# Twenty-four extra rows on SyncE's queue between two tile loads of a batch norm

## The chip, the cores and the metric

The kernel runs on one core of a Trainium2 chip. The metric is the device time of one execution in microseconds, and the time of a kernel is the median of its runs.

## The reference

The input `x` has the shape (32, 256, 128, 128) in float32. Each of the 256 channels is normalized with given statistics, so the whole computation is one multiplication and one addition per element with numbers that depend on the channel alone:

```python
def reference(x, gamma, beta, running_mean, running_var):
    eps = 1e-5
    ...  # each parameter reshaped to (1, 256, 1, 1)
    return gamma * (x - mean) / np.sqrt(var + eps) + beta
```

The input has 537 MB and the output as much.

## The kernel before

The channels are put on the 128 partitions, so `x` becomes 64 tiles (`NT`) of 128 rows; a row is one channel of one image, 16384 numbers or 64 KiB, and a tile is 8 MiB. Three tiles (`NBUF` = 3) fit in the on-chip memory, as `bufs[0]` to `bufs[2]`; tile i uses buffer i modulo 3 and is changed in place.

Loads are issued by SyncE on its queue (q1 in the profile), stores by ScalarE on its own (q10). Both queues are served by the same 16 DMA engines. At the start SyncE issues, in this order: the left half of tile 0 (L90, semaphore `early`), the four parameter vectors into `rows`, 16 rows of 1 KiB each (L93), the right half of tile 0 (L97, `first[0]`), and tiles 1 and 2 whole (L99, `first[1]` and `first[2]`). None of these waits for anything, except that the first parameter load waits for the memset of `rows` (L91). While the data come in, VectorE and ScalarE turn the parameters into `scale_t` and `shift_t`, one column for each half of the channels (L109 to L126).

For each later tile VectorE handles the first columns in two instructions (L132: 1696 columns, then up to 14976) and ScalarE the rest (L143); for tile 0 VectorE takes the left half and ScalarE the right. ScalarE then waits for VectorE's part and issues the store of the tile (L171). Before its part of tile i it waits until the store of tile i - 1 has landed, except for tile 0 and the last two (L168). SyncE's loop over the later loads (L161 to L164) waits for two things: the buffer's old tile must be stored (`gone(i - NBUF)`), and VectorE must have done the first part of tile i - 1 (`vfirst`), which needs that tile's load to have landed. So in mid-run about one load and one store are under way at any time.

Tile 0 is not treated until its halves have landed: VectorE's first part waits for `early`, ScalarE's for `first[0]`. Tile 2 is awaited by VectorE and ScalarE through `first[2]`.

Of the kernel before, what the change touches and what calls it, by code (L numbers as in the profile page):

```python
# [10 lines left out]
NHEAD = 3  # L11
VFIRST = 1696
VMOST = 14976
VHEAD = 8192
VLAST = 9216


@with_exitstack
def kernel(
# [9 lines left out]
    nc = tc.nc  # L29
# [14 lines left out]
    xr = x.rearrange("n (cb p) h w -> (n cb) p (h w)", p=P)  # L44
# [5 lines left out]
    bufs = [data.tile([P, HW], f32, name=f"t{s}", tag=f"t{s}") for s in range(NBUF)]  # L50
# [12 lines left out]
    loaded = [tc.alloc_semaphore(f"loaded{s}") for s in range(NBUF)]  # L63
    stored = [tc.alloc_semaphore(f"stored{s}") for s in range(NBUF)]
    early = tc.alloc_semaphore("early")
    first = [tc.alloc_semaphore(f"first{s}") for s in range(NHEAD)]
    vfirst = tc.alloc_semaphore("vfirst")
    vdone = tc.alloc_semaphore("vdone")
# [5 lines left out]
    with tc.tile_critical():  # L74
# [20 lines left out]
                inst._wait_ge(vec, zeroed)  # L95
            inst.then_inc(fetched, 16)
        nc.sync.dma_start(out=bufs[0][:, right], in_=xr[0][:, right]).then_inc(first[0], 16)  # L97
        for i in range(1, NHEAD):
            nc.sync.dma_start(out=bufs[i][:], in_=xr[i]).then_inc(first[i], 16)  # L99

        def landed(i):
            if i < NHEAD:
                return first[i], 16
            s = i % NBUF
            before = 1 if s < NHEAD else 0
            return loaded[s], 16 * (i // NBUF + 1 - before)
# [6 lines left out]
        for q in range(NQ):  # L113
# [3 lines left out]
            out=std_t[:],  # L117
            in_=var_t,
# [11 lines left out]
        def vector_part(i, first_col, end):  # L130
            t, cb = bufs[i % NBUF], i % NCB
            return nc.vector.tensor_scalar(  # L132
                out=t[:, first_col:end],
                in0=t[:, first_col:end],
                scalar1=scale_t[:, cb : cb + 1],
                scalar2=shift_t[:, cb : cb + 1],
                op0=mybir.AluOpType.mult,
                op1=mybir.AluOpType.add,
            )

        def scalar_part(i, first_col):
            t, cb = bufs[i % NBUF], i % NCB
            return nc.scalar.activation(  # L143
                out=t[:, first_col:],
                in_=t[:, first_col:],
                func=mybir.ActivationFunctionType.Identity,
                bias=shift_t[:, cb : cb + 1],
                scale=scale_t[:, cb : cb + 1],
            ).then_inc(adone, 1)

        def gone(i):
            return stored[i % NBUF], 16 * (i // NBUF + 1)
# [3 lines left out]
        for i in range(1, NT):  # L156
            vector_part(i, 0, VFIRST)._wait_ge(*landed(i)).then_inc(vfirst, 1)
            vector_part(i, VFIRST, VLAST if i == last else VMOST).then_inc(vdone, 1)

# [6 lines left out]
        for i in range(NT):  # L166
            if 0 < i < NT - 2:
                nc.scalar.wait_ge(*gone(i - 1))  # L168
            scalar_part(i, VHEAD if i == 0 else VLAST if i == last else VMOST)._wait_ge(*landed(i))
            nc.scalar.wait_ge(vdone, i + 1)  # L170
# [37 lines left out]
```

## Time and profile before

| | |
|---|---|
| median of 3 runs | 2485.43 us (2484.16 to 2489.99) |
| the profiled execution | 2487.8 us, with a span of 2486.0 us |
| VectorE busy | 526.0 us (21%), 138 instructions |
| ScalarE busy | 111.8 us (4%), 66 instructions |
| moved by DMA | 1073.85 MB, mean 432 GB/s over the span |
| packets on q1 (loads) | 9488, 536.94 MB |
| packets on q10 (stores) | 9216, 536.88 MB |
| a tile's load or store, median from issue to landing | 37.4 us or 37.0 us |
| half of tile 0, issue to landing | 16.4 us |

The span goes from the first to the last instruction of the core; the profiled execution's own time has 1.8 us around it. The row of digits marked DMA gives the mean busy share of the 16 DMA engines in 40 equal slices of the span, in tenths. In a list of waits, each line has the engine and line that waited, what it waited for, the sum in us, how often, and the longest. In a table of windows, the columns are the stretch, its length, the busy time of each engine with its number of instructions, the clock, the share of DMA and the GB/s moved. The trace also holds one record for each single transfer of a DMA engine, with its queue, start, duration and size; a whole row of a tile is one such transfer of 64 KiB.

### The profile page before, as it was taken

What the parts mean: (1) busy time and instruction counts of PE and PEld (TensorE: products, weight loads), DVE (VectorE), ACT (ScalarE), POOL (GpSimd) and SP (SyncE); (2) the same over time, 40 slices, a digit from 0 to 9 for tenths busy, and PEclk for the clock granted to TensorE, in tenths of its full rate; (3) what the DMA queues carried; (4) which work ended last, traced back from release to release, by engine and by line L of the source; (5) the groups of instructions that cost most, each with busy time, mean ns of one, the idle gap of its engine ahead of it and who ended that gap; (6) DMA issues with size and microseconds to landing.
All of it is one profiled execution on the core that took longest, in us unless ns stands there. A gap on an engine that the chain in (4) does not pass through costs nothing.

```text
span 2486.0 us, 578 instructions
## 1 busy us (share of the span) xinstructions
DVE 526.0 (21%) x138; ACT 111.8 (4%) x66; POOL 0.2 (0%) x4
## 2 busy tenths in 40 slices
DVE  2121221221212212122121221212212122121220
ACT  1000000000000000000000000000000000000001
POOL 0000000000000000000000000000000000000000
DMA  9999999999999999999999999999999999999999
GB/s 406 428 431 438 433 428 439 437 433 429 438 429 432 437 436 427 433 432 433 433 438 428 437 436 427 437 436 428 434 437 437 428 437 437 431 433 436 437 429 405
DMA packets 18708, 1073.85 MB, mean 432 GB/s; under 512 B 2128, under 2 KB 2192, under 8 KB 2192
## 3 DMA queue, kind: packets, MB, share of 16 engines
q1 hardware_dynamic: 9488, 536.94, 50.1%
q10 hardware_dynamic: 9216, 536.88, 49.8%
q14 instruction: 4, 0.03, 0.0%
HBM read 536.94 MB, written 536.87 MB: 432 GB/s over the span
## 4 chain that ended last, share of the span: by engine, by line
DMA 93%; DVE 4%; another core or an unknown queue 2%; ACT 0%; issue 0%; SPq 0%; DVEq 0%
DMA t<-in_x_dram 92%; DVE t L132 3%; DMA rows<-in_running_mean_dram 0%; ACT t L143 0%; DVE turned L110 0%; SPq L93 0%; DVE rows L91 0%; DVE par L114 0%; ACT std_t L116 0%; DVE rstd_t L123 0%; DVE shift_t L126 0%; DVE scale_t L124 0%; DVE ms_t L125 0%; DVE eps_t L109 0%
## 5 line engine op out<-in xcount | busy, mean ns | idle before, releaser
L132 DVE TENSOR_SCALAR t<-t,scale_t,shift_t 128x13280 f32<-128x13280 f32 (+2 forms) x127 | 522.5, 4156 | 1921.4 <-DMA t<-in_x_dram 1921.3
L143 ACT ACTIVATE t<-t,shift_t,scale_t 128x1408 f32<-128x1408 f32 (+1 forms) x64 | 110.3, 1723 | 2335.6 <-DMA out_dram<-t 2272.5
L110 DVE STREAM_TRANSPOSE turned<-rows 32x1024 f32<-32x1024 f32 x1 | 1.2, 1232 | 11.8 <-DMA rows<-in_running_mean_dram 11.8
L116 ACT ACT_TABLE_LOAD x1 | 1.3, 1283 | 0.9 <-SPq L74 0.9
L91 DVE MEMSET rows<- 32x1024 f32 x1 | 0.9, 912 | 1.2 <-SPq L74 1.2
L116 ACT ACTIVATE std_t<-par,eps_t 128x2 f32<-128x2 f32 x1 | 0.3, 295 | 14.0 <-DVE par L114 14.0
L114 DVE COPY par<-turned 32x8 f32<-32x8 f32 x4 | 0.6, 162 | 0.1
L123 DVE RECIPROCAL rstd_t<-std_t 128x2 f32<-128x2 f32 x1 | 0.2, 166 | 0.4 <-ACT std_t L116 0.4
L124 DVE TENSOR_TENSOR scale_t<-par,rstd_t 128x2 f32<-128x2 f32 x1 | 0.2, 161 | 0.0
L126 DVE TENSOR_TENSOR shift_t<-par,ms_t 128x2 f32<-128x2 f32 x1 | 0.2, 161 | 0.0
L125 DVE TENSOR_TENSOR ms_t<-par,scale_t 128x2 f32<-128x2 f32 x1 | 0.2, 160 | 0.0
L192 POOL MEMSET const-bfloat16-1.0<- 128x1 bf16 x1 | 0.1, 101 | 0.0
L192 POOL MEMSET const-uint8-127<- 128x1 uint8 x1 | 0.1, 101 | 0.0
L192 POOL MEMSET const-float32-0.0<- 128x1 f32 x1 | 0.1, 98 | 0.2 <-issue 0.2
L192 POOL MEMSET const-float32-1.0<- 128x1 f32 x1 | 0.1, 98 | 0.0
L109 DVE MEMSET eps_t<- 128x1 f32 x1 | 0.1, 59 | 0.1
## 6 DMA issues: line engine op xcount, KB each, us to landing
t<-in_x_dram SPq DMA_DIRECT2D x2, 4096.0 KB, 16.4
out_dram<-t ACTq DMA_DIRECT2D x64, 37.0
t<-in_x_dram SPq DMA_DIRECT2D x63, 37.4
rows<-in_running_var_dram SPq DMA_DIRECT2D x1, 16.0 KB, 11.2
rows<-in_gamma_dram SPq DMA_DIRECT2D x1, 16.0 KB, 11.0
rows<-in_beta_dram SPq DMA_DIRECT2D x1, 16.0 KB, 10.8
rows<-in_running_mean_dram SPq DMA_DIRECT2D x1, 16.0 KB, 10.6
```

Source lines behind the costliest of these rows:

```text
L91: zeroed = step(nc.vector.memset(rows[:], 0.0))
L109: step(nc.vector.memset(eps_t[:], eps))
L110: step(nc.vector.transpose(out=turned[:], in_=rows[:]), fetched, 16 * NPAR)
L114: placed = step(nc.vector.tensor_copy(out=flat[q * B : (q + 1) * B], in_=blocks[:, :, q, 0]))
L116: nc.scalar.activation(out=std_t[:], in_=var_t, func=mybir.ActivationFunctionType.Sqrt, bias=eps_t[:], scale=1.0,)._wait_ge(vec, placed).t ...
L123: step(nc.vector.reciprocal(out=rstd_t[:], in_=std_t[:]), act, 1)
L124: step(nc.vector.tensor_mul(out=scale_t[:], in0=gamma_t, in1=rstd_t[:]))
L125: step(nc.vector.tensor_mul(out=ms_t[:], in0=mean_t, in1=scale_t[:]))
L126: ready = step(nc.vector.tensor_sub(out=shift_t[:], in0=beta_t, in1=ms_t[:]))
L132: return nc.vector.tensor_scalar(out=t[:, first_col:end], in0=t[:, first_col:end], scalar1=scale_t[:, cb : cb + 1], scalar2=shift_t[:, cb ...
L143: return nc.scalar.activation(out=t[:, first_col:], in_=t[:, first_col:], func=mybir.ActivationFunctionType.Identity, bias=shift_t[:, cb : ...
L192: nc = _bacc.Bacc("TRN2", target_bir_lowering=False, num_devices=1)
```

## The change

Between the load of tile 0's right half and the load of tile 1, SyncE issues three small loads into the buffer of tile 2. Each takes a quarter of a row (4096 numbers, 16 KiB) from every fourth row: 12 rows of the first quarter, 8 rows of the second, 4 rows of the third. They bring the same data to the same places as tile 2's whole load does later. Each has a semaphore of its own, and SyncE waits for all three before it issues the load of tile 2, which is now a statement of its own behind the loop. The rest of the kernel is the same.

```diff
+GROUPS = (12, 8, 4)
+PIECE = 4096
...
     early = tc.alloc_semaphore("early")
+    aside = [tc.alloc_semaphore(f"aside{g}") for g in range(len(GROUPS))]
...
         nc.sync.dma_start(out=bufs[0][:, right], in_=xr[0][:, right]).then_inc(first[0], 16)
-        for i in range(1, NHEAD):
+        rest = NHEAD - 1
+        for g, k in enumerate(GROUPS):
+            cut = slice(g * PIECE, (g + 1) * PIECE)
+            nc.sync.dma_start(
+                out=bufs[rest][0 : 4 * k : 4, cut], in_=xr[rest][0 : 4 * k : 4, cut]
+            ).then_inc(aside[g], 16)
+        for i in range(1, rest):
             nc.sync.dma_start(out=bufs[i][:], in_=xr[i]).then_inc(first[i], 16)
+        for g in range(len(GROUPS)):
+            nc.sync.wait_ge(aside[g], 16)
+        nc.sync.dma_start(out=bufs[rest][:], in_=xr[rest]).then_inc(first[rest], 16)
```

## The prediction

> **What bounds the kernel.** I read the page first: how busy each engine is, what the DMA engines moved over the span, and the two queues' shares.
>
> ```profile
> span 2486.0 us, 578 instructions
> ...
> DVE 526.0 (21%) x138; ACT 111.8 (4%) x66; POOL 0.2 (0%) x4
> ...
> DMA  9999999999999999999999999999999999999999
> ...
> q1 hardware_dynamic: 9488, 536.94, 50.1%
> q10 hardware_dynamic: 9216, 536.88, 49.8%
> ```
>
> VectorE and ScalarE are mostly idle; the 16 DMA engines are busy for 50.1 + 49.8 = 99.9% of the span, half with loads (q1, SyncE's queue), half with stores (q10, ScalarE's). One DMA engine therefore moves 536.88 MB / 16 in 0.498 x 2486 us of stores, 27.1 GB/s. The trace's records of single transfers say the same: a 64 KiB row takes 2418 ns, which no row of either direction undercuts, and 97% of the 16256 rows are within 3 ns of that. The kernel is bound by each DMA engine's own speed.
>
> Then the waits of the compute engines and of SyncE, and the chain at the end, to see whether a late DMA engine can leave others without work.
>
> ```profile
> DVE t L132 <- DMA t<-in_x_dram: 1921.3, 63, 35.4
> ...
> SPq L163 <- DMA out_dram<-t: 1427.0, 61, 68.9
> SPq L164 <- DVE t L132: 958.4, 61, 16.0
> ```
>
> ```profile
> 2413.45 42.43 DMA t<-in_x_dram
> 2455.88 0.03 issue
> 2455.90 6.36 ACT t L143
> ```
>
> Everybody waits for transfers. In mid-run a load starts at 1020.27 us and a store at 1045.02, the next load 39 us after the first: the two boundaries lie 25 and 14 us apart, so where one queue runs dry for a moment the other has at least 14 us of rows left. Only the last store is different: it is issued at 2462.29, when ten of the sixteen engines had been idle for about 0.5 us; these end at 2482.5, the latest at 2484.3.
>
> Last, how much time is lost to rows slower than 2418 ns, because a change of order can win only that. The windows show one such stretch, the start of tile 1's load.
>
> ```profile
> 23.50:34.35 10.85, 0.00 (x0) 7.21 (x1) 0.00 (x0) 1.00 1.00 387
> 1990.00:2240.00 250.00, 55.12 (x13) 9.36 (x6) 0.00 (x0) 1.00 1.00 433
> ```
>
> The last column is GB/s: 387 while all 16 engines read in step (five rows each at about 2714 ns, begun within 0.5 us of each other), 433 in a stretch without slow rows. Over the whole run the rows above 2418 ns cost 5.4 us per DMA engine: 1.5 in those five rows, the rest nearly all in loads (later loads 3.7). With every row at its least the data need 16256 / 16 x 2.418 + 16 x 1.213 (tile 0's half rows) = 2476.1 us; the first starts 2.0 us into the span, the span ends 1.7 us after the last, and the profiled execution is 2487.8 us against a span of 2486.0. That gives a floor of 2481.6 on the profiled execution, 6.2 below it. This execution lies 2.4 us above the median of 2485.43 and inside the runs' 2484.16 to 2489.99; I carry differences over to the median.
>
> **The change, part by part.**
>
> *Three more DMAs.* They add 24 rows of 16 KiB, 393 KB on 1073.85 MB. At 27.1 GB/s a row is 0.60 us of one engine. Spread evenly that is 1.5 rows, 0.9 us; all on one engine it is 14.5 us. Nearest row: the four parameter loads, 16 rows of 1 KiB each, show 64 packets of 46 ns that start within 1.0 us in all; one engine alone would need 2.9 us, so rows are dealt out over the engines. I take one row per engine: 12 engines get one row, 8 of them a second, 4 a third. Four DMA engines then have 1.8 us more to do, four 1.2, four 0.6, four nothing. [...]
>
> *What the 1.8 us cost at the end.* An engine with 1.8 us more ends 1.8 us later, unless it was one of the early ones: ends differ by 1.8 us and the early ones had 0.5 us idle, so the cost is 0 if the lag falls on early engines and 1.8 if on late ones. Who is late is made by slow reads along the way and I cannot tell it; I take 1.2.
>
> *SyncE's issues and its waits.* Three more issues of about 0.4 us (L93's duration) put tile 1's load at about 5.7 us instead of 4.4. That is covered: its rows cannot start before tile 0's right half is done at 23.5 us. SyncE then waits for all three pieces, which sit directly behind tile 0's right half and land at about 26 us; tile 2's load is queued behind this wait, and all later loads. It goes out at some 27 us instead of 4.9, behind tile 1's load, which keeps each engine busy from 24 to 26 us on for eight rows: cover to 43 us at least, 16 us to spare. The store of tile 0 (31.79 us) is on another queue. [...] ScalarE's start on tile 0 does not move, as the pieces lie behind the half it waits for.
>
> *The five slow rows.* They ran with 0.5 us between first and last engine; now the groups are 0.6 us apart. If closeness made them slow, 1.5 us comes back; if reading alone did, nothing. I take half, -0.7. [...]
>
> *Slow reads later.* After 100 us a read that begins with 8 or more engines reading and ends with fewer than 12 of them costs 22 ns over 2418 on the mean of 2417 such reads; all others 1.2 ns. An engine that alternates reads and writes, 0.6 us behind the next group, makes the two later of four groups end their reads while the others write, so they pay 22 ns per read. But each payment pushes the engine further back, and after some 2.4 us it reads where most others write and pays nothing: the loss ends itself. The run before, which starts in step, is spread over the whole row by 600 us and paid 3.7 us in this way. I take a little more, +0.6, with bounds of -3.7 (no slow reads) and +7.4 (the later groups never drift out: 504 reads x 22 ns = 11.1 us, less 3.7).
>
> Sum: 1.2 - 0.7 + 0.6 = +1.1 us; 2487.8 to 2488.9 for the profiled execution, 2485.43 to **2486.5** for the median. A difference of 0.3% (7.5 us) is about what a measurement of this kernel can tell from no change.
>
> **The rivals.**
>
> *Gain.* The shift takes the slow rows away: -1.5 and -3.7 with +1.2 of lag, -4.0 us, 2481.4. For it: 1.5 of the 2.2 us lost in the first 250 us fell into rows that began within 0.5 us of each other. Against it: 1990 to 2240 us has no slow row although eleven of the sixteen engines stay within 0.7 us of each other there (rows under way at 2000 us), and the stretches with slow reads are ones in which the engines were spread. Even all of it stays under 0.3%; more than that needs a base that itself ran like the slowest of its three (2489.99).
>
> *Slower: the later groups stay where they pay.* +7.4 + 1.8 = +9.2, 2494.6. It decides from about 85% of the reads of the last group: (7.5 - 1.8 + 3.7) / 11.1. For it: reads are slow exactly at a half-and-half mix, which the shift sets up on purpose from the start, and the engines with most extra bytes are the last group. Against it: the drift just told.
>
> *The pieces are not dealt out* as taken, many rows falling on one engine: up to +14.5 us, 2499.9. Against it stand the parameter rows.
>
> *The shift is there but dies at once*, since the first slow reads move engines by as much as it does (one read took 3869 ns): 2485.4 to 2487.2. I count this with the forecast.
>
> **How the numbers follow.** Forecast 0.44 (2484 to 2489, all within 0.3%); gain 0.28, of which 0.06 beyond 0.3%; later groups stay 0.22, of which 0.18 beyond 0.3%; rows on few engines 0.06. So faster 0.06, same 0.44 + 0.22 + 0.04 = 0.70, slower 0.18 + 0.06 = 0.24. The range goes from 2480.5, just under the gain, to 2495, just over the price of the staying groups; outside remain the rows on few engines and the ends of the other cases.
>
> **What would show it.** In the profile after: tile 1's load issue at about 5.7 us and tile 2's at about 27 us; three issues of 192, 128 and 64 KB landing by 27 us; GB/s in the first 11 us of tile 1's load between 387 and 433; the DMA row still 9 everywhere; the spread of the engines' last ends 2 to 4 us. The prediction is wrong if mean GB/s in mid-run is under 430 with slow reads throughout, if rows run below 2418 ns, or if DMA engines stand idle while SyncE waits at the new waits.

## The result: 0.19% slower, and a profile that does not show why

The changed kernel has a median of 2490.68 us against 2485.36 us for the kernel before, 22 runs each. The ratio is 1.0019 with a 95% interval of 1.0013 to 1.0025, that is 4.7 us (3.2 to 6.2). It is inside the range and within 0.3%, but four times the +1.1 us of the sum. Here and below a median is over all runs of a kernel, while a ratio compares only the runs within 1.5% of their kernel's fastest, which leaves out, among others, four of the six of big_64k, two of the six of equal_64k and three of the twelve of after_v0 (2563 to 2566 us, not profiled).

First the page and the start of the timeline of the profile after. In the timeline the columns are the start in us, the duration, the engine, the line and the instruction.

```profile
span 2485.8 us, 582 instructions
...
DMA  9999999999999999999999999999999999999999
...
q1 hardware_dynamic: 9536, 537.33, 50.1%
q10 hardware_dynamic: 9216, 536.88, 49.8%
```

```profile
4.41 2.24 SPq L104 DMA_DIRECT2D t<-in_x_dram  x3
6.69 0.44 SPq L108 DMA_DIRECT2D t<-in_x_dram  x1
...
26.00 0.33 SPq L111 DMA_DIRECT2D t<-in_x_dram  x1
31.25 0.37 ACTq L183 DMA_DIRECT2D out_dram<-t  x1
```

The DMA engines are busy for the same 99.9%. The 48 more packets (9536 for 9488) are the 24 rows of 16 KiB and 24 records of 4 bytes: the trace has 12, 8 and 4 semaphore steps for the three DMAs, where the load of tile 1 has 16. Twelve of the 24 rows were under way at once at 23.2 us, so they were dealt out over the engines; that it was one row of a DMA per engine, as the prediction took it, fits these counts. The three issues took 2.24 us in place of the 1.3 that I had put, so tile 1's load goes out at 6.69 us and not at 5.7; tile 2's goes out at 26.00, near the 27 forecast. The start of tile 1's load and the last store, in windows (the last two columns are the busy share of the DMA engines and GB/s), and SyncE's new wait:

```profile
23.50:34.35 10.85, 0.00 (x0) 7.21 (x1) 0.00 (x0) 1.00 0.99 426
```

```profile
2455.00:2467.00 12.00, 5.27 (x2) 6.36 (x1) 0.00 (x0) 1.00 0.88 382
```

```profile
SPq L110 <- DMA t<-in_x_dram: 18.8, 1, 18.8
```

426 GB/s stand for the 387 of before: the five slow rows are gone. SyncE's 18.8 us at L110 hold up nothing, as tile 1's rows were queued (DMA share 1.01 from 26 to 36 us). At the end the DMA engines are busy for only 88% of the 12 us around the last store; the same window of the kernel before has:

```profile
2455.00:2467.00 12.00, 5.27 (x2) 6.36 (x1) 0.00 (x0) 1.00 1.00 431
```

These two profiled executions, 2487.8 us before and 2487.56 after, cannot show the loss: one lies above its kernel's median and one below. So I made an account of each profiled execution from the records of single transfers, as a mean per DMA engine: work (all rows at 2418, 1213 or 611 ns for 64, 32 or 16 KiB), what slow rows took beyond that, and idle time. (The 7.3 us of slow rows of the kernel before are the prediction's 5.4, which counted rows of 64 KiB alone, and 1.9 in tile 0's half rows.) With 2.4 to 2.8 us for the ends of the program the terms add up to the measured time in all of them, which makes them comparable. The column "offset" is the time from a store's issue to the next load's landing, read in mid-run; it becomes important below.

| kernel | offset, us | time, us | work | slow rows | idle before the last store | idle elsewhere |
|---|---|---|---|---|---|---|
| before | 12.9 | 2487.80 | 2476.1 | 7.3 | 0.3 | 1.7 |
| changed | 12.9 | 2487.56 | 2477.0 | 4.7 | 1.2 | 2.2 |
| equal_16 | 17.7 | 2488.03 | 2477.9 | 4.5 | 2.6 | 0.5 |
| late_60 | 12.9 | 2483.99 | 2477.0 | 2.2 | 0.5 | 1.8 |
| small_1024 | 8.0 | 2483.92 | 2476.3 | 3.3 | 0.0 | 1.8 |
| held_3 | 22.5 | 2493.58 | 2476.1 | 10.2 | 4.3 | 0.4 |
| after_v0 | 8.0 | 2486.05 | 2477.0 | 4.8 | 0.0 | 1.7 |
| equal_v0 | 8.0 | 2487.04 | 2477.9 | 4.7 | 0.0 | 1.8 |
| before_v0 | 0.8 and 3.2 in turn | 2585.16 | 2476.1 | 81.9 | 0.0 | 24.4 |
| big_64k | 22.5 | 2535.58 | 2479.7 | 39.3 | 8.5 | 5.4 |
| equal_64k | 22.6 | 2544.85 | 2483.3 | 46.0 | 9.1 | 3.6 |

### The profile page after: what moved, and what is told of

Its sections match the earlier page's. It is cut to its first block, busy times and chain, and to the rows that moved or that the text cites. A ratio compares the mean times of both kernels' runs of the same rounds, so it can differ in the third digit from the quotient of the medians.

```text
span 2485.8 us, 582 instructions
## 1 busy us (share of the span) xinstructions
DVE 526.0 (21%) x138; ACT 111.8 (4%) x66; POOL 0.2 (0%) x4
## 3 DMA queue, kind: packets, MB, share of 16 engines
q1 hardware_dynamic: 9536, 537.33, 50.1%
## 4 chain that ended last, share of the span: by engine, by line
DMA 93%; DVE 4%; another core or an unknown queue 2%; ACT 0%; issue 0%; SPq 0%; DVEq 0%
DMA t<-in_x_dram 92%; DVE t L144 3%; DMA rows<-in_running_mean_dram 0%; ACT t L155 0%; DVE turned L122 0%; SPq L96 0%; DVE rows L94 0%; DVE par L126 0%; ACT std_t L128 0%; DVE rstd_t L135 0%; DVE shift_t L138 0%; DVE ms_t L137 0%; DVE scale_t L136 0%; DVE eps_t L121 0%
```

## The first four experiments: is it the shift, the place, or the issues?

**equal_16**: the same three DMAs, but 16 rows in each.

```diff
-GROUPS = (12, 8, 4)
+GROUPS = (16, 16, 16)
```

> Three pieces of 16 rows each in place of 12, 8 and 4: the same three issues, the same wait ahead of tile 2's load, but every DMA engine gets the same 48 KiB (1.8 us) more, so nothing is shifted between the engines. Theory 'lag' (the change costs what the engines with most extra rows have more to do, 1.8 us): 1.8 us over the kernel before. Theory 'slow reads' (the shift between the engines makes more reads slow over the whole run): 1.8 us over before as well, with slow rows as before, the five slow rows at the start of tile 1's load back. Rival 'queue' (the three issues and SyncE's wait cost the time, whoever gets the rows): as the changed kernel, about 5 us over before.

Measured: median 2490.09 us against 2484.09, ratio 1.0023 (1.0014 to 1.0031). No engine is shifted against another and the loss is as large. The shift is not needed for a loss of this size, which speaks against my main rival, the groups that stay where they pay. Part of the loss is a dearer piece: the 48 rows of 16 KiB took 1112 ns on the mean, most 1234 to 1279, twice the 611 ns of the fastest. In late_60, whose 24 pieces of the same size go from device memory to device memory, each took 611. That points to the on-chip side, though those 24 also ran at another time, among other rows. What doubles them was not shown. Three such pieces are 3.3 us per engine where 1.8 had been put, still 2.4 short of the measured 5.7 (the ratio times 2484).

**late_60**: the pieces ahead of tile 60's load, from the input to the output's last tile.

```diff
+            if i == WHEN:        # 60, ahead of the load of tile i
+                for g, k in enumerate(GROUPS):
+                    cut = slice(g * PIECE, (g + 1) * PIECE)
+                    nc.sync.dma_start(
+                        out=outr[last][0 : 4 * k : 4, cut], in_=xr[last][0 : 4 * k : 4, cut]
+                    ).then_inc(aside[g], 16)
...
+            if i == last:
+                for g in range(len(GROUPS)):
+                    nc.scalar.wait_ge(aside[g], 16)
```

> The pieces of 12, 8 and 4 rows are moved from the start to just ahead of tile 60's load, and go from the input to the output's last tile in device memory (overwritten by the last store), so that no load waits for them. The engines are shifted only for the last 6% of the run. 'Lag': 1.8 us over before. 'Slow reads': also about 1.8 us, the remaining 3 us of the changed kernel's loss are gone, since no time is left for slow reads. If the loss is made at the end alone (the last store waits for the latest engine and the shift is paid more than once): about 5 us over before.

Measured: median 2487.64 against 2484.09, ratio 1.0021 (1.0012 to 1.0030), 3.0 to 7.5 us. That is over the 1.8 us of both first theories, by at least 1.2. Its profiled execution, at 2483.99, is the fastest of its eleven and shows nothing of it. What the run does say: a loss of this size does not need 2400 us to build up.

**small_1024**: the same issues and waits, 4 KiB a row.

```diff
-PIECE = 4096
+PIECE = 1024
```

> Pieces of 4 KiB a row in place of 16 KiB: the same issues and waits, a shift of at most 0.45 us between the groups of engines, in the order of the 0.5 us that they differ by anyway. 'Lag': 0.45 us over before, less up to 1 us if the five slow rows go: within 1 us of before. 'Slow reads': close to before too, as the groups stay in step at first. 'Queue': about 5 us over before.

Measured: median 2485.14, ratio 1.0004 (0.9995 to 1.0013). Three issues and SyncE's wait cost nothing that can be told from zero (3.2 us at most by the interval); the cover named in the prediction holds. Its account has no idle time before the last store. Its last load landed at 2449.4 us and its last store went out at 2455.8, and the window around both is full:

```profile
2440.00:2470.00 30.00, 5.27 (x2) 6.36 (x1) 0.00 (x0) 1.00 1.01 437
```

For equal_16, whose last load landed at 2457.8 us and whose last store went out at 2464.2, a window over both reads:

```profile
2455.00:2467.00 12.00, 5.27 (x2) 6.36 (x1) 0.00 (x0) 1.00 0.70 300
```

**big_64k**: whole rows.

```diff
-PIECE = 4096
+PIECE = 16384
...
-            cut = slice(g * PIECE, (g + 1) * PIECE)
+            cut = slice(g, g + 4 * k, 4)
...
-                out=bufs[rest][0 : 4 * k : 4, cut], in_=xr[rest][0 : 4 * k : 4, cut]
+                out=bufs[rest][cut], in_=xr[rest][cut]
```

> Pieces of whole rows, 64 KiB in place of 16 KiB: the groups are shifted by 2.4, 4.8 and 7.2 us, one row each. 'Lag': 7.2 us over before. 'Slow reads': the groups with one and with three rows read while the others write; half of the reads run at a half-and-half mix: 508 reads times 12 to 20 ns, 6 to 10 us of slow reads per engine in place of 3.7, and 7.2 of lag, so 10 to 14 us over before. 'Queue': 5 us over before as in the changed kernel.

Measured: median 2552.55 (2509.67 to 2595.30), 68 us over before; the ratio, 1.0154 (1.0110 to 1.0198), is 38 us (27 to 49). Every theory was far too low. Slow rows took 39.3 us per engine in the profiled execution and idle time 14, while the extra work is 3.6.

**What the timelines had in common.** In small_1024, before and equal_16, around 2010 us, the store's issue (ACTq) and VectorE's start on the next landed load:

```profile
2011.45 0.34 ACTq L183 DMA_DIRECT2D out_dram<-t  x1
2019.49 8.27 DVE L144 TENSOR_SCALAR t<-t,scale_t,shift_t 128x1696 f32<-128x1696 f32 x2 [30.38 <-DMA t<-in_x_dram]
```

```profile
2013.01 0.34 ACTq L171 DMA_DIRECT2D out_dram<-t  x1
2025.87 8.27 DVE L132 TENSOR_SCALAR t<-t,scale_t,shift_t 128x1696 f32<-128x1696 f32 x2 [30.37 <-DMA t<-in_x_dram]
```

```profile
2008.75 0.34 ACTq L183 DMA_DIRECT2D out_dram<-t  x1
2026.45 8.27 DVE L144 TENSOR_SCALAR t<-t,scale_t,shift_t 128x1696 f32<-128x1696 f32 x2 [30.37 <-DMA t<-in_x_dram]
```

The landing comes 8.0, 12.9 and 17.7 us after the store's issue: steps of 4.8 us, one row of each direction (2 x 2418 ns). Within the first 90 us the offset takes one of these values, and in these three it keeps it to the end, since loads and stores both come round every 38.7 us. The larger it is, the later the last load lands against the stores that could fill its time, and the longer the engines idle before the last store (0.0, 0.3 to 1.2 and 2.6 us in the table). From this came a new theory, "offset": the extra rows lie on the loads' queue alone and push the loads' boundaries back against the stores'. These profiles alone do not show it: before and the changed kernel have the same 12.9, and at 12.9 the slow rows differ by 5.1 us from one execution to another (2.2 in late_60, 7.3 in before).

## Four experiments on the offset

**held_3**: no extra rows; the kernel before with one load held once.

```diff
             nc.sync.wait_ge(*gone(i - NBUF))
+            if i == NHEAD:
+                nc.sync.wait_ge(vdone, i)
```

> No extra rows at all: the kernel before, in which SyncE holds the first load of its loop (tile 3) until VectorE has finished tile 2, some 7 us more, once. New theory 'offset', formed from the traces: what counts is by how much the loads' boundaries lie behind the stores'. The time from a store's issue to the next load's landing was 12.9 us before and with the change, 8.0 with 4 KiB pieces and 17.7 with equal pieces, in steps of one row of each direction (4.8 us), and stayed the same from the second load to the end; the larger it is, the longer all DMA engines idle before the last store (mean 0.3, 1.2, 0.0 and 2.6 us). 'Offset' expects 17.7 or 22.5 us here from the start to the end, 2 to 5 us of idle engines before the last store, and 2 to 5 us over before. 'Lag' and 'slow reads', in which the extra rows or the shift between engines cost the time, expect no difference, since there are neither.

Measured: median 2491.39 against 2484.42, ratio 1.0028 (1.0018 to 1.0037). The offset was 8.0 us until the hold, went to 22.5 and stayed:

```profile
2007.90 0.34 ACTq L173 DMA_DIRECT2D out_dram<-t  x1
2030.91 8.27 DVE L132 TENSOR_SCALAR t<-t,scale_t,shift_t 128x1696 f32<-128x1696 f32 x2 [30.80 <-DMA t<-in_x_dram]
```

A loss of 7 us (4.5 to 9.2), where 2 to 5 were expected, with the same bytes, pieces and order of engines, and with only 0.4 us of idle time elsewhere, so the hold itself is not what is paid: the place of the loads against the stores costs time by itself. The theory had put it all at the end; the account shows 4.3 us there, and 10.2 us of slow rows, spread over the whole run.

**after_tail and before_tail**: the last tile in two halves of columns, each with its own load, computation and store.

```diff
+            if i == last:
+                nc.sync.wait_ge(vfirst, i - 1)
+                for h, cut in enumerate((left, right)):
+                    nc.sync.dma_start(out=bufs[s][:, cut], in_=xr[i][:, cut]).then_inc(tail[h], 16)
+                continue
...
+        for h, cut in enumerate((left, right)):
+            scalar_part(last, h * HW // 2 + VTAIL, (h + 1) * HW // 2)._wait_ge(tail[h], 16)
+            nc.scalar.wait_ge(vdone, last + 1 + h)
+            nc.scalar.dma_start(out=outr[last][:, cut], in_=bufs[last % NBUF][:, cut])
...
```

> The changed kernel, with the last tile loaded, computed and stored in two halves of its columns, so that the left half's store is there when the older stores run out. 'Offset': the idle time before the last store is gone, and what is left over the kernel before with the same tail is the lag of 1.8 to 2 us; so 2 to 4 us below the changed kernel. 'Slow reads': the loss of about 5 us stays.

> The kernel before with the same tail in two halves, as the base for the run beside it. 'Offset': at an offset of 12.9 us it saves only the idle time of 0.3 us per engine and may lose as much by more, smaller rows: within 1 us of before. All theories agree here; it is needed for the difference.

Measured: 2491.20 with ratio 1.0025 (1.0017 to 1.0034), and 2485.90 with 1.0010 (1.0002 to 1.0019). The loss stayed, as "slow reads" had said and "offset" had not. But the test was weaker than planned: in after_tail (offset 17.7) the left half's store ran out before the right half had landed and been computed, and 2.4 us of idle time per engine were left. It shows that such a tail is no cure; it decides nothing on the cause. The two profiles are worth more for their starts, which are those of the kernel before and of the changed kernel. The first two lines are before_tail, the last two after_tail:

```profile
1817.92 0.34 ACTq L179 DMA_DIRECT2D out_dram<-t  x1
1826.66 8.27 DVE L133 TENSOR_SCALAR t<-t,scale_t,shift_t 128x1696 f32<-128x1696 f32 x2 [31.05 <-DMA t<-in_x_dram]
```

```profile
1815.20 0.34 ACTq L191 DMA_DIRECT2D out_dram<-t  x1
1833.20 8.27 DVE L145 TENSOR_SCALAR t<-t,scale_t,shift_t 128x1696 f32<-128x1696 f32 x2 [30.66 <-DMA t<-in_x_dram]
```

In mid-run the offset is 8.0 us in before_tail (8.7 in this one cycle) and 17.7 in after_tail (18.0 in this one). So one kernel does not have one offset: the start of the kernel before gave 12.9 us twice (before, late_60) and 8.0 twice (before_tail, held_3 until its hold), that of the changed kernel 12.9 and 17.7.

**equal_64k**: whole rows, 16 in each DMA.

```diff
-GROUPS = (12, 8, 4)
+GROUPS = (16, 16, 16)
```

(beside the edit of big_64k)

> Pieces of whole rows as in the run with 64 KiB pieces (68 us over before), but 16 rows in each, so that every DMA engine gets the same three rows and none is shifted. Three rows are 7.3 us, or up to twice that, since 16 KiB pieces from 16 rows took 1.11 us in place of 0.61; and the load boundary may go one or more steps back. 'Shift by whole rows makes slow reads': 8 to 20 us over before, few slow rows. If the bytes or the late load of tile 2 are behind the 68 us: again 30 us or more.

Measured: median 2537.89, 53 us over before; the ratio, 1.0160 (1.0137 to 1.0183), is 40 us (34 to 45). Equal rows lose as unequal ones do, so the shift between engines is not behind big_64k's loss either. The second extra row of every engine took 5.09 to 5.11 us, twice the 2.418 of a tile's row, as the 16 KiB pieces of equal_16 took twice their 611 ns. Both kernels have an offset of 22.5 us and more, but held_3 has that too at a sixth of the loss. The start explains little: after the first 124 us slow rows still cost 34 us in big_64k and 31 us in equal_64k, and what makes them stays open.

## Putting the offset back

**after_v0 and before_v0**: ScalarE takes tile 0 from column 2688, so the first store goes out later; 4.8 us were planned, and it went out at 35.80 us for 31.25 in after_v0 and at 35.30 for 31.79 in before_v0.

```diff
-VHEAD = 8192
+VHEAD = 2688
...
+        nc.scalar.wait_ge(early, 16)
         for i in range(NT):
```

> The changed kernel, with ScalarE taking tile 0 from column 2688 on instead of 8192, so that the first store goes out some 4.8 us later (ScalarE needs about 12 us for it) while the loads stay as they are; the DMA engines have the loads of tiles 1 and 2 to do meanwhile. 'Offset' (in the form left by the last runs: the loads' boundaries lying further behind the stores' cost time, by slow reads and by idle engines at the end): the offset goes down by one step of 4.8 us against the changed kernel's own, and the time to about 2 us over the kernel before, what the lag costs: 2486 to 2488. 'Lag' and 'slow reads from the shift': no change against the changed kernel, 2489 to 2491.

> The same 2688 columns in the kernel before, without the extra rows. 'Offset': one step down from 12.9 or 8.0 us to 8.0 or 3.2; as fast as the kernel before or up to 2 us faster. 'Lag' and 'slow reads from the shift': as the kernel before.

Measured for after_v0: median 2485.89 against 2484.37, ratio 1.0002 (0.9992 to 1.0012). With all the extra rows, issues, waits and the shift in place, the 4.7 us are down to 0.5 (-2.0 to 3.0), no loss that can be told from zero. The offset is 8.0 us, and no engine idles before the last store:

```profile
2013.49 0.34 ACTq L184 DMA_DIRECT2D out_dram<-t  x1
2021.50 8.27 DVE L144 TENSOR_SCALAR t<-t,scale_t,shift_t 128x1696 f32<-128x1696 f32 x2 [30.38 <-DMA t<-in_x_dram]
```

Measured for before_v0: median 2585.16, ratio 1.0399 (1.0386 to 1.0412), 100 us slower where 0 to 2 us of gain or nothing was expected. Its timeline, the waits of SyncE and the page's GB/s:

```profile
1209.43 0.34 ACTq L172 DMA_DIRECT2D out_dram<-t  x1
1212.64 8.27 DVE L132 TENSOR_SCALAR t<-t,scale_t,shift_t 128x1696 f32<-128x1696 f32 x2 [33.38 <-DMA t<-in_x_dram]
...
1250.92 0.34 ACTq L172 DMA_DIRECT2D out_dram<-t  x1
1251.68 8.27 DVE L132 TENSOR_SCALAR t<-t,scale_t,shift_t 128x1696 f32<-128x1696 f32 x2 [30.77 <-DMA t<-in_x_dram]
```

```profile
SPq L163 <- DMA out_dram<-t: 2182.3, 61, 72.1
SPq L164 <- DVE t L132: 295.0, 61, 6.0
```

```profile
DMA packets 18708, 1073.85 MB, mean 416 GB/s; under 512 B 2128, under 2 KB 2192, under 8 KB 2192
```

Now the loads land 3.2 and 0.8 us after the store's issue, in turn. The boundaries of both queues fall together: SyncE's loop waits 2182 us for stores, where it was 1427, and 295 us for loads (through VectorE), where it was 958; engines that have no row of either queue idle for 24 us, and slow rows, this time as many stores as loads, take 82. So a later first store is no gain of its own: it pays in the changed kernel and ruins the kernel before, in step with where it puts the boundaries.

**equal_v0**: equal_16 with the same later store.

> The pieces of 16 rows each (no shift between the engines; 5.7 us over before at an offset of 17.7 us) with the first store some 4.8 us later, as in the run that took the changed kernel back to before. 'Offset': one step down, to 12.9 us, and the time to 2486 to 2488, 2 to 4 us over before: the 3.3 us of the pieces and about as little idle time as in before. If the late store helped only because the engines were shifted: 2490 as without it.

Measured: median 2487.40 against 2485.24, ratio 1.0011 (1.0002 to 1.0020), where equal_16 had 1.0023. The loss is 2.7 us (0.5 to 5.0) for 5.7 (3.5 to 7.7), near the 3.3 us of the pieces; the two intervals overlap, so that it shrank is likely and not shown. The offset went two steps down, to 8.0, where one was expected, and no engine idles before the last store:

```profile
2014.26 0.34 ACTq L184 DMA_DIRECT2D out_dram<-t  x1
2022.30 8.27 DVE L144 TENSOR_SCALAR t<-t,scale_t,shift_t 128x1696 f32<-128x1696 f32 x2 [30.36 <-DMA t<-in_x_dram]
```

If it helped, it did so without any shift of the engines.

**after_again**: the changed kernel once more, unaltered.

> The changed kernel once more, for one more profile: its first one had an offset of 12.9 us and a time of 2487.56, under its median of 2490.68. 'Offset' expects the executions to differ by their offset: 12.9 us again with about 2488, or 17.7 or 22.5 us with 2489 to 2494 and the excess in slow reads or in idle engines before the last store. 'Slow reads from the shift' expects a slower execution to have more slow reads at the same offset.

Measured: one execution of 2488.04 us, with an offset that starts at 12.9 and falls to 8.0 by 700 us, against the expectation that it stays; 6.1 us of slow rows, no idle time before the last store. Like the first profile it lies under the kernel's median. The first expectation is met in its time alone (12.9 us with about 2488), and the slower execution that the second one needs was not caught.

## Why the prediction was right in sign and range and wrong in size

*What the sum was worth*: little. It named 2486.5 us, with 2484 to 2489 for the case that it describes, and the median is 2490.68. The range holds it because its upper part was there for the later groups that stay where they pay, which is not what happened; that the range was met is in part luck.

*What bounds the kernel*: right. No row ran below 2418 ns, and work, slow rows and idle time account for every profiled execution but for the 2.4 to 2.8 us of its ends. The gain rival was bounded rightly, as no version beat the kernel before by anything that can be told.

*Issues and waits, covered and without a term in the sum*: right, as far as the interval of small_1024 goes.

*The pieces, 0.60 us each*: the term was undersized. They took 838 ns on the mean in the changed kernel (0.61 to 1.14 us) and 1112 in equal_16, for 611 in late_60, where they go to device memory; the cause was not shown. The 0.60 us had been worked out from the DMA engines' rate on whole rows alone (27.1 GB/s).

*The lag at the end, +1.2*: not contradicted, and not shown. In the changed kernel's profile the engines' last ends are spread over 2.0 us (2 to 4 forecast), but in the kernel before over 1.8, and one engine was late, not a group of four; after_v0, with all of the lag, leaves room for it (-2.0 to 3.0 us). One reading was off: the engines that idled for about 0.5 us in the kernel before did so after the last store's issue at 2462.29, until its first rows at 2463.2, and not before it.

*The five slow rows, -0.7*: the step failed in its cause. They went, and the first 124 us lost 0.6 us to slow rows of 64 KiB in place of 1.7. But late_60 and before_tail, whose starts are those of the kernel before, lost 0.9 and 0.6 there: the slow start belonged to that one execution. In held_3 the 16 engines began tile 1 within 0.6 us of each other, nearly as close as the 0.5 of before, and their first rows took 2418 to 2428 ns, not the 2708 of before.

*Slow reads later, +0.6, and the rival that the last groups keep paying*: both looked to the shift, and equal_16 shows as large a loss without any, after_v0 the shift without a loss. After 100 us slow rows cost 2.9 us in the changed kernel's profile against 3.7 before.

*What was missing*: the prediction saw the two boundaries, "25 and 14 us apart", and took them as mere cover. They are a state. Extra rows on the loads' queue ahead of the steady part can move it; held_3 shows that moving it far costs, after_v0 that moving it back takes the loss away as far as can be told, and equal_v0 agrees within its noise. By this the rest of some 3 us is the price of the offset, a term that the sum did not have; that is argued from these runs, not read off a profile.

Open: which offsets the changed kernel has where it takes its median time or more, since both its profiles (12.9, and 12.9 falling to 8.0) lie 2.6 us and more under the median, and so does the one at 17.7 of after_tail (2487.15 of 2491.20); and whether slow rows or idle time make up the loss. The link to the offset rests on interventions, not on a profile that shows the loss. Late_60's excess is unexplained for the same reason.

## What to carry to other kernels

When two queues share the same DMA engines and each keeps one transfer in flight, ask not only how many bytes a change adds but on which queue and before which boundary: read the time from a store's issue to the next load's landing in both profiles. A start that is moved by a few us can cost more for the rest of the run than the bytes (100 us in before_v0, whose first store goes out 3.5 us later and which moves not a byte more), and the same remedy that repairs one kernel can ruin its neighbour (ratios of 1.0002 and 1.0399 here). Two single profiles cannot explain a difference as small as the scatter of executions; add up work, slow rows and idle time of each first.

## What the runs showed of the hardware

In the kernel before the engines took rows of the two queues in turn where both had some: from 1990 us on, 1 load and 15 stores started in one stretch of 2.42 us and 15 loads and 1 store in the next, 16 rows of each in 4.84 us. The offsets seen in mid-run (3.2, 8.0, 12.9, 17.7 and 22.5 us, beside the 0.8 of before_v0) lie such steps apart. With boundaries 0.8 to 3.2 us apart in before_v0 the mean was 416 GB/s for 432, and stores, at 2418.2 ns on the mean in the kernel before and 2418.1 in the changed one, lost as much there as loads (43 and 38 us per engine). Rows of 16 KiB four partitions apart, 16 in a DMA, took 1112 ns on the mean in equal_16, most 1234 to 1279, for 611 of the fastest. In the changed kernel the three strided DMAs of 4 to 12 rows took SyncE 0.59 to 0.91 us each to issue, the loads of tiles 1 and 2, 128 rows each, 0.44 and 0.33.
